# Classical FFN weights: the remainder made by a negation on ScalarE and an accumulating transfer

## The chip, the cores and the metric

The kernel runs on one core of one Trainium2 chip. A core has five engines with a queue of instructions each: TensorE (PE in the profile, with its weight loads as PEld), VectorE (DVE), ScalarE (ACT), GpSimd (POOL) and SyncE (SP). Each queue is worked off in order, and the engines wait for one another through semaphores. DMA transfers are issued from the queues of SP, ACT or POOL and run on 16 DMA engines that all queues share. Data lies in SBUF (128 partitions); matrix products land in PSUM.

The metric is the time of one execution on the device in microseconds (us), lower is better; of several runs the median is taken.

## The reference

One decoder layer on x of 512 tokens by 1024 features, in float32: a half-step SwiGLU feed-forward block, a mixing block with a diagonal state-space model beside sliding-window attention, a second half-step SwiGLU block and a final RMS norm.

```python
def swiglu(h, w_gate, w_up, w_down):
    return (jax.nn.silu(h @ w_gate) * (h @ w_up)) @ w_down

x = x + 0.5 * swiglu(rms_norm(x, ffn1_norm), ffn1_w_gate, ffn1_w_up, ffn1_w_down)
...
x = x + y @ w_out
x = x + 0.5 * swiglu(rms_norm(x, ffn2_norm), ffn2_w_gate, ffn2_w_up, ffn2_w_down)
return rms_norm(x, final_norm)
```

`w_gate` and `w_up` are 1024 by 2816, `w_down` is 2816 by 1024: 22 blocks of 128 columns or rows.

## The kernel before

**Three products for one.** PE multiplies in a format with fewer bits than float32 (fp32r). So every operand is split into a high part, rounded to fp32r, and a remainder, operand minus high part, and `mm3` adds three products into one PSUM tile: weight-high by x-high (L182), weight-high by x-remainder (L183), weight-remainder by x-high (L184).

**Weights.** `weight` (L175) takes a tile of 128 partitions by up to 1024 columns: eight blocks of 128 by 128 for a gate or up column block, six or five for a down tile. `weight_part` (L169) loads it from SP's queue into `wraw`, casts it on ScalarE into `whi` (L154, inside `copy`), and has DVE subtract `whi` from `wraw` into `wlo` (L173). Each of the three names has three buffers, so the cast of a tile waits until PE has read `whi` of the tile three before for the last time, and the load of a raw tile until the buffer of the tile three before has been read by L173. A gate or up tile is 24 matmuls, a down tile 18 or 15.

**Who calls it.** `weight` and `weight_part` have an argument `key`. The mixing block passes a name for each of its weights (`u0`, `wkv1`, `out00` and so on), and a table of engines, `ENGINES`, sends a few of these splits to GpSimd. The feed-forward blocks pass nothing, so `key` is the empty string: in the first block all 44 gate and up tiles and 32 down tiles, in the second block the 12 tiles of the first six column blocks and 24 down tiles. The remaining ten column blocks of the second block go another way (`pairs`, with its own cast L536, subtraction L537 and sums on GpSimd L502), and so does the last group of its down tiles. `start` (L288) loads x and the first gate and up tile in three cuts each, by calling `weight_part` itself.

**What else runs beside it.** In the first feed-forward block, after each tile one step of a list (`prep_steps`) is put into the program. These steps prepare the state-space matrices: short operations on DVE, then two long chains of products and sums on GpSimd (`tt` with the engine G, all at L635), one for `aB`, which PE later transposes (`tV`, L830, four empty steps behind the chain), and one for `matC`, which is read much later, in the mixing block. Before the last column blocks of the second feed-forward block, GpSimd adds weight blocks (`s`, L502) for `pairs`.

**The order.** The source writes a tile's load, cast and subtraction just ahead of its matmuls. The framework's planner reorders the instructions with a simulated timeline: an instruction goes into its engine's queue when the planner reckons it ready, earlier in the source first. It allots buffers, and adds the semaphore waits. On the chip each queue then runs in that fixed order.

Of the kernel before, what the change touches and what calls it, by code (L numbers as in the profile page):

```python
# [10 lines left out]
F32 = mybir.dt.float32  # L11
# [3 lines left out]
ALU = mybir.AluOpType  # L15
AX = mybir.AxisListType

P = 128
# [116 lines left out]
class Body:  # L135
# [33 lines left out]
    def weight_part(self, tiles, src, c0, c1, key=""):  # L169
        raw, hi, lo = (t[:, c0:c1] for t in tiles)  # L170
        self.nc.sync.dma_start(raw, src[:, c0:c1])
        self.copy("hi" + key, hi, raw)
        self.eng("lo" + key).tensor_tensor(lo, raw, hi.bitcast(F32), op=ALU.subtract)  # L173

    def weight(self, src, cols, key=""):  # L175
        t = self.weight_tiles()
# [3 lines left out]
    def mm3(self, out, wh, wl, xh, xl, start, stop, **kw):  # L180
        mm = self.nc.tensor.matmul
        mm(out, wh, xh, start=start, stop=False, **kw)  # L182
        mm(out, wh, xl, start=False, stop=False, **kw)  # L183
        mm(out, wl, xh, start=False, stop=stop, **kw)  # L184
        if self.small:
            self.small.pop(0)()
# [101 lines left out]
    def start(self):  # L288
        nc = self.nc
        self.prenorm(self.g_ffn1)  # L290
        self.x = [self.cp.tile([P, 512], F32, name=f"x{k}") for k in range(KT)]
        src = self.d["wgu1"][0]
        ws = [self.weight_tiles() for _ in range(2)]
        cuts = {0: (0, 2), 2: (2, 5), 5: (5, 8)}
        for k in range(KT):
            nc.sync.dma_start(self.x[k], self.d["xT"][k])
            if k in cuts:
                for gu in range(2):
                    self.weight_part(ws[gu], src[gu].rearrange("p k m -> p (k m)"), cuts[k][0] * P, cuts[k][1] * P)
            self.xg.append(self.split_gain(self.x[k], self.g_ffn1[:, k:k + 1]))  # L300
        self.first = [(w[1], w[2]) for w in ws]

# [1235 lines left out]
```

## Time and profile before

| | us |
|---|---|
| median of 3 runs | 935.81 |
| lowest and highest run | 926.32, 936.68 |
| span of the profiled execution | 925.4 |
| the profiled execution's own time (span and what lies around it) | about 926.3 |

The profiled execution's time is taken to be that of the run next to its span. The profile is one execution. Its page gives the busy time of each engine, the span in 40 slices, the chain of work that ended last, the costliest groups of instructions by line, and the DMA issues; a group's last column is the idle time of its engine ahead of it and what ended that. The trace behind it answers questions for one engine, tile, line or stretch of time, always in microseconds from the start of the span; "L173" is line 173 of the kernel, and "x3" means three instructions in one row. A matmul's row is longer (0.39 us) than the distance to the next (0.23 us), since matmuls overlap.

### The profile page before, as it was taken

The page shows a single profiled execution, that of the slowest core. Times are in us where ns is not written, and L with a number is a line of the kernel's source. Part 1 is how long each engine was busy: PE and PEld are TensorE (multiplying, and loading weights), DVE is VectorE, ACT ScalarE, POOL GpSimd, SP SyncE. Part 2 cuts the span into 40 slices and gives each one's busy share as a digit, 9 for nine tenths or more (in the row PEclk, how much of TensorE's full clock was granted, in tenths as well). Part 3 has the DMA queues.
Part 4 walks back from the last instruction along what each step waited for, and adds up shares of the span by engine and source line. Part 5 has one row for each costly group of instructions (what it writes and reads, how often), then busy time and mean ns, then how long its engine had stood idle before and what let it go on. Part 6 is the DMA issues. An engine that isn't in the chain of part 4 may idle for free.

```text
span 925.4 us, 13303 instructions
## 1 busy us (share of the span) xinstructions
PE 907.5 (98%) x5036; PEld 772.9 (84%) x5036; DVE 624.0 (67%) x1167; ACT 369.2 (40%) x660; POOL 314.9 (34%) x272
## 2 busy tenths in 40 slices
PE   9999999999999999999979999999999999999996
PEld 6887888888888888888868887888899889988995
DVE  7886444474464443958896787697588459855966
ACT  7142233222232322622487433543355335532553
POOL 0009902179950000501231063180553055404502
PEclk9999999999999999999989999999999999999998
DMA  7332423243213321547201122215421442135112
GB/s 244 125 92 53 153 91 103 64 133 121 84 57 112 114 76 56 164 149 186 78 1 46 46 79 104 91 36 157 150 86 35 134 156 87 35 110 180 47 47 91
DMA packets 37503, 91.92 MB, mean 99 GB/s; under 512 B 8032, under 2 KB 10304, under 8 KB 37184
## 3 DMA queue, kind: packets, MB, share of 16 engines
q1 hardware_dynamic: 37008, 90.54, 31.3%
q8 instruction: 39, 0.64, 0.3%
q10 hardware_dynamic: 432, 0.55, 0.2%
q14 instruction: 24, 0.20, 0.1%
HBM read 87.44 MB, written 3.64 MB: 98 GB/s over the span
## 4 chain that ended last, share of the span: by engine, by line
PE 91%; DVE 5%; ACT 2%; issue 1%; DMA 1%; SPq 0%; DVEq 0%; ACTq 0%
PE gu L182 11%; PE gu L183 11%; PE gu L184 11%; PE dn L182 9%; PE dn L183 8%; PE dn L184 8%; PE gua L184 3%; PE gua L183 3%; PE gua L182 3%; PE guc L184 2%; PE guc L182 2%; PE guc L183 2%; PE ow L182 2%; PE ow L183 2%; PE ow L184 2%; PE pt L1037 1%
## 5 line engine op out<-in xcount | busy, mean ns | idle before, releaser
L154 ACT CAST whi<-wraw 128x1024 fp32r<-128x1024 f32 (+4 forms) x134 | 122.6, 921 | 307.6 <-PE gu L183 118.9
L173 DVE TENSOR_TENSOR wlo<-wraw,whi 128x1024 fp32r<-128x1024 f32 (+4 forms) x133 | 155.4, 1173 | 42.6 <-ACT whi L154 42.5
L182 PE MATMUL gu<-hi,whi 128*128 128x512 f32 x448 | 178.9, 402 | 1.5 <-ACT hi L195 1.4
L183 PE MATMUL gu<-lo,whi 128*128 128x512 f32 x448 | 176.7, 395 | 0.1
L184 PE MATMUL gu<-hi,wlo 128*128 128x512 f32 x448 | 176.3, 395 | 0.0
L183 PE MATMUL dn<-lo,whi 128*128 128x512 f32 (+1 forms) x336 | 130.1, 389 | 0.0
L182 PE MATMUL dn<-hi,whi 128*128 128x512 f32 (+1 forms) x336 | 130.1, 392 | 0.0
L184 PE MATMUL dn<-hi,wlo 128*128 128x512 f32 (+1 forms) x336 | 128.9, 389 | 0.0
L182 PEld LDWEIGHTS gu<-hi,whi 128*128 128x128 f32 x448 | 84.4, 189 | 21.8 <-ACT hi L195 2.3
L184 PEld LDWEIGHTS gu<-hi,wlo 128*128 128x128 f32 x448 | 84.3, 188 | 19.7
L183 PEld LDWEIGHTS gu<-lo,whi 128*128 128x128 f32 x448 | 84.5, 189 | 19.2 <-DVE lo L197 1.0
L182 PEld LDWEIGHTS dn<-hi,whi 128*128 128x128 f32 x336 | 63.3, 188 | 14.9 <-ACT whi L154 1.1
L184 PEld LDWEIGHTS dn<-hi,wlo 128*128 128x128 f32 x336 | 63.2, 188 | 14.2
L183 PEld LDWEIGHTS dn<-lo,whi 128*128 128x128 f32 x336 | 63.3, 188 | 13.6
L269 POOL TENSOR_TENSOR sq<-sq 128x512 f32<-128x512 f32 x17 | 25.1, 1476 | 139.9 <-ACT sq L265 137.2
L537 DVE TENSOR_TENSOR wlo<-s,whi 128x512 fp32r<-128x512 f32 x64 | 55.2, 904 | 12.2 <-ACT whi L536 12.0
L502 POOL TENSOR_TENSOR s<-s,wraw 128x512 f32<-128x512 f32 x32 | 50.4, 1576 | 33.9 <-DMA wraw<-wgs 32.9
L502 POOL TENSOR_TENSOR s<-wb 128x512 f32<-128x512 f32 x16 | 23.6, 1474 | 112.3 <-DMA wb<-wgs 91.4
L345 DVE TENSOR_TENSOR u<-gu,R 128x512 f32<-128x512 f32 x28 | 19.2, 685 | 48.2 <-PE gu L184 48.2
L412 DVE SCALAR_TENSOR_TENSOR x<-dn,x 128x512 f32<-128x512 f32 x32 | 21.7, 685 | 42.7 <-PE dn L184 42.7
L536 ACT CAST whi<-s 128x512 fp32r<-128x512 f32 x64 | 36.5, 618 | 30.4 <-issue 9.3
L428 DVE SCALAR_TENSOR_TENSOR x<-dn,x 128x512 f32<-128x512 f32 x24 | 16.5, 690 | 46.2 <-PE dn L184 46.2
(371 smaller groups left out, 2030.1 us busy)
## 6 DMA issues: line engine op xcount, KB each, us to landing
wraw<-wgu SPq DMA_DIRECT2D x54, 512.0 KB, 3.4
wraw<-wd SPq DMA_DIRECT2D x40, 384.0 KB, 3.2
wb<-wgs SPq DMA_DIRECT2D x32, 256.0 KB, 5.2
wraw<-wgs SPq DMA_DIRECT2D x16, 512.0 KB, 3.7
wraw<-wd SPq DMA_DIRECT2D x16, 320.0 KB, 2.9
wraw<-wout SPq DMA_DIRECT2D x8, 512.0 KB, 3.4
x<-xT SPq DMA_DIRECT2D x8, 256.0 KB, 5.1
wraw<-wu SPq DMA_DIRECT2D x4, 512.0 KB, 3.3
```

Of the source, the lines that this page charges most:

```text
L154: (e.copy if e is self.nc.scalar else e.tensor_copy)(out, x)
L173: self.eng("lo" + key).tensor_tensor(lo, raw, hi.bitcast(F32), op=ALU.subtract)
L182: mm(out, wh, xh, start=start, stop=False, **kw)
L183: mm(out, wh, xl, start=False, stop=False, **kw)
L184: mm(out, wl, xh, start=False, stop=stop, **kw)
L269: (eng or b.nc.gpsimd).tensor_tensor(self.acc, self.acc, sq, op=ALU.add)
L345: nc.vector.tensor_tensor(u, pu, self.R, op=ALU.mult)
L412: nc.vector.scalar_tensor_tensor(self.x[m], ps, 0.5, self.x[m], op0=ALU.mult, op1=ALU.add)
L428: self.nc.vector.scalar_tensor_tensor(self.x[m], ps, 0.5, self.x[m], op0=ALU.mult, op1=ALU.add)
L502: add = lambda o, x, y: nc.gpsimd.tensor_tensor(o, x, y, op=ALU.add)
L536: self.chained("A", lambda: A.copy(hi[:, c], w))
L537: self.chained("V", lambda: V.tensor_tensor(lo[:, c], w, hi[:, c].bitcast(F32), op=ALU.subtract))
```

## The change

For tiles with an empty `key`, the remainder is no longer a subtraction on DVE. ScalarE, which has just written `whi`, reads it again and writes its negative into `wlo`. Then a DMA from GpSimd's queue moves `wraw` into `wlo` and adds it to what stands there: minus the high part, plus the raw weight. The first two tiles, which `start` loads in cuts, get the key `"0"`, and so keep cast and subtraction as they were. The weights of the mixing block have keys of their own and are unchanged, as is the path through `pairs`. So 110 tiles change: 54 of 1024 columns, 40 of 768 and 16 of 640.

```diff
@@ weight_part
         self.copy("hi" + key, hi, raw)
-        self.eng("lo" + key).tensor_tensor(lo, raw, hi.bitcast(F32), op=ALU.subtract)
+        if key:
+            self.eng("lo" + key).tensor_tensor(lo, raw, hi.bitcast(F32), op=ALU.subtract)
+        else:
+            self.nc.scalar.mul(lo, hi.bitcast(F32), -1.0)
+            self.nc.gpsimd.dma_start(lo, raw, accum_op=ALU.add)
@@ start
-                    self.weight_part(ws[gu], src[gu].rearrange("p k m -> p (k m)"), cuts[k][0] * P, cuts[k][1] * P)
+                    self.weight_part(ws[gu], src[gu].rearrange("p k m -> p (k m)"), cuts[k][0] * P, cuts[k][1] * P, "0")
```

## The prediction

> **What bounds the kernel now.** I read the page first (busy shares, slices, chain of work, groups, DMA issues).
>
> ```profile
> span 925.4 us, 13303 instructions
> PE 907.5 (98%) x5036; PEld 772.9 (84%) x5036; DVE 624.0 (67%) x1167; ACT 369.2 (40%) x660; POOL 314.9 (34%) x272
> ...
> POOL 0009902179950000501231063180553055404502
> ...
> PE 91%; DVE 5%; ACT 2%; issue 1%; DMA 1%; SPq 0%; DVEq 0%; ACTq 0%
> ...
> L154 ACT CAST whi<-wraw 128x1024 fp32r<-128x1024 f32 (+4 forms) x134 | 122.6, 921 | 307.6 <-PE gu L183 118.9
> L173 DVE TENSOR_TENSOR wlo<-wraw,whi 128x1024 fp32r<-128x1024 f32 (+4 forms) x133 | 155.4, 1173 | 42.6 <-ACT whi L154 42.5
> ...
> wraw<-wgu SPq DMA_DIRECT2D x54, 512.0 KB, 3.4
> wraw<-wd SPq DMA_DIRECT2D x40, 384.0 KB, 3.2
> ...
> wraw<-wd SPq DMA_DIRECT2D x16, 320.0 KB, 2.9
> ```
>
> PE is busy 98% and is 91% of the chain: only 17.9 us of the span are not matmul, so no relief of another engine is worth more than that. GpSimd, 34% on average, is nearly full in slices 3, 4 and 9, 10 (23 us each): the first feed-forward block. Then I read whom PE and the DMA queue wait for.
>
> ```profile
> PE pt L1329 <- ACT pr L1308: 4.7, 1, 4.7
> ...
> PE gua L184 <- DVE wlo L537: 0.3, 1, 0.3
> ...
> SPq L171 <- DVE wlo L173: 492.9, 104, 32.3
> ```
>
> PE loses nothing to L173. The loads of raw weights wait on it 104 times: a raw buffer comes free when its remainder is made. That is where the lead of a weight tile is set, and it reads from the casts, each released by PE's last L183 on the tile three before.
>
> ```profile
> 199.53 0.83 ACT L154 CAST whi<-wraw 128x768 fp32r<-128x768 f32 x1 [3.36 <-PE dn L183]
> 203.69 0.84 ACT L154 CAST whi<-wraw 128x768 fp32r<-128x768 f32 x1 [3.32 <-PE dn L183]
> ...
> 231.69 1.05 ACT L154 CAST whi<-wraw 128x1024 fp32r<-128x1024 f32 x1 [4.55 <-PE gu L183]
> 237.29 1.05 ACT L154 CAST whi<-wraw 128x1024 fp32r<-128x1024 f32 x1 [4.54 <-PE gu L183]
> ...
> 291.41 0.73 ACT L154 CAST whi<-wraw 128x640 fp32r<-128x640 f32 x1 [3.65 <-PE dn L183]
> 294.43 0.73 ACT L154 CAST whi<-wraw 128x640 fp32r<-128x640 f32 x1 [2.29 <-PE dn L183]
> ```
>
> PE takes 5.6 us for a gate/up tile (1024 columns), 4.2 for a down tile of six blocks (768), and here 3.0 for one of five (640). With three buffers a cast begins two tiles ahead of PE's need, plus about 0.7 us (the last L184 and the two matmuls before the next first one): a lead of 11.9, 9.1 and 6.7 us. Today cast and subtraction fill about 2.2 us of it.
>
> **What is removed and added.** 54 + 40 + 16 = 110 subtractions leave DVE, at most 129 us at the group's mean of 1.17. PE does not get them: it waits for none of them above. ScalarE gains 110 negations of the cast's size, 54 x 1.05 + 40 x 0.84 + 16 x 0.73 = 102 us on an engine busy 40%: hidden, except that each lengthens the way to its remainder. A negation needs the remainder's buffer, free at PE's last L184, one matmul after the cast's release and long before the cast ends, so it adds no wait of its own; the casts and Silus behind it on ScalarE come 0.7 to 1.05 us later, and of these one is in the sum below. The first two tiles keep the DVE form. What matters is the new transfer: no row shows an accumulating one, or any DMA from GpSimd.
>
> ```profile
> L171 SPq DMA_DIRECT2D wraw<-wd x56: 327/328/949, 50.9 to 828.1; - x56
> ...
> L173 POOL TENSOR_TENSOR wlo<-wraw,whi 128x1024 fp32r<-128x1024 f32 x3 | 7.4, 2466 | 42.6 <-ACT whi L154 42.4
> ...
> matT<-dz SPq DMA_DIRECT2D x2, 1024.0 KB, 8.3
> ...
> 206.00:267.00 61.00, 61.00 (x263) 49.05 (x263) 30.73 (x30) 15.33 (x18) 60.92 (x44) 1.00 0.31 94
> ```
>
> Its issue lies between 0.33 us (SP's) and 2.47 (a GpSimd pass over the tile); I take the middle, 1.4, since GpSimd has no hardware issue in this trace to be nearer to. Its transfer lies between the plain load (3.4 us for 512 KB) and the slowest row with twice the bytes, 8.3. An add must read its destination as well, so I take twice the bytes at the loads' slope: from 320 to 512 KB they grow 0.5 us, 1.3 us per 512 KB, giving 4.7, 4.2 and 3.7 us. DMA is 31% busy, worth 0.5; a cast or Silu ahead on ScalarE 0.6. From the end of the negation that is an estimate of 7.2, 6.7 and 6.2 us (bounds 3.7 and 11). What is left of the lead after cast and negation is 9.8, 7.4 and 5.2: hidden by 2.6 and 0.7, and 1.0 us short for tiles of five blocks. On "Collectives: The Full Stack" (section on the bandwidth ceiling) the Trainium skill says that a DMA reduction runs at about half the rate of a copy because it reads two sources; no run here shows it yet. With plain loads' transfer instead the terms below marked * vanish, and the sum would be about 12 instead of 24.
>
> The raw loop also grows: cast 0.84, negation 0.84, 6.7, SP's issue 0.33, load 3.2 is 11.9 us against three tiles of 12.6. It holds, barely. SP's queue is in order, so what stands behind a waiting raw load (the x tiles, the pair weights of the second block) waits too; in the paired stages that is the load that L502 needs.
>
> **Start.** The third tile is the first new one.
>
> ```profile
> 14.55 1.05 ACT L154 CAST whi<-wraw 128x1024 fp32r<-128x1024 f32 x1 [0.59 <-DMA wraw<-wgu]
> ...
> 18.57 0.39 PE L184 MATMUL gu<-hi,wlo 128*128 128x512 f32 x1
> ```
>
> Cast to 15.6, negation to 16.65, plus 7.2 is 23.85, and PE wants it at 18.57: 5.3 late, or 1.6 if the planner moves the eight L184 behind the sixteen others of the tile. I take 4.
>
> **GpSimd's queue.** Its work is in order, so each issue delays the work behind it, and each waits for what is ahead.
>
> ```profile
> 70.50 0.62 POOL L635 TENSOR_TENSOR tB<-sB,p_zi 128x256 f32<-128x256 f32 x1
> 71.08 1.34 POOL L635 TENSOR_TENSOR tB<-sB,p_zr 128x256 f32<-128x256 f32 x1
> ...
> 113.22 1.45 POOL L635 TENSOR_TENSOR aB<-tB 128x256 f32<-128x256 f32 x2
> 115.11 0.60 PE L830 MATMUL tV<-cst,aB 128*128 128x128 f32 x4
> ...
> 220.97 1.06 POOL L635 TENSOR_TENSOR tC<-matC,s_ar 128x512 f32<-128x512 f32 x1
> 221.58 1.54 DVE L173 TENSOR_TENSOR wlo<-wraw,whi 128x1024 fp32r<-128x1024 f32 x1 [0.16 <-ACT whi L154]
> 221.99 2.04 POOL L635 TENSOR_TENSOR tC<-Y,s_ai 128x512 f32<-128x512 f32 x1
> ```
>
> The chain that builds aB runs from about 70 to 114.67, and PE's transposes read it at 115.11: 0.4 us of slack. Ten tiles fall into that stretch: 10 x 1.4 = 14 us of issues. Against it stands what DVE gives back: beside L173 a GpSimd operation stretches (1.06 to 2.04 us; 0.62 to 1.34), so ten vanished subtractions return about 7. The chain ends 7 later and PE waits for it, in order, unless its transposes are moved: I take 6. The Trainium skill ("SBUF — State Buffer", who interferes with whom) has the rule behind that give-back, that a DVE instruction with two SBUF inputs blocks a GpSimd one that reads SBUF; the rows agree.
>
> The second burst (206 to 267, 60.92 us busy) has no reader soon. But some eight down tiles of six blocks fall into the two bursts, and their transfers queue behind operations of 1 to 2 us: half an operation, 0.8, uses up the 0.7 of margin, and behind two of them a tile is 2 late: 4* in all. An issue that stands ahead of its negation's end holds back everything behind it; the planner puts it where it reckons it ready, so I count none (rival D). The sixteen tiles of five blocks are 1.0 short, paid once per three buffers, and each wait counts again: 16 x 0.33 = 5*.
>
> **Second block.** Down tiles after the two paired stages:
>
> ```profile
> 717.21 0.83 ACT L154 CAST whi<-wraw 128x768 fp32r<-128x768 f32 x1 [0.19 <-PE gua L183]
> ...
> 723.30 0.40 PE L184 MATMUL dn<-hi,wlo 128*128 128x512 f32 x1
> ...
> 796.31 1.75 POOL L502 TENSOR_TENSOR s<-s,wraw 128x512 f32<-128x512 f32 x1
> 798.54 0.69 DVE wlo L537
> ```
>
> Negated at 718.9, plus 6.7 is 725.6 against 723.3: 2.3 late, twice, 5*. The sums of L502 feed a piece of the chain itself (798.54); a transfer placed among them costs its issue once or twice: nothing if none is, 3 at most, I take 0.
>
> Sum: 4 + 6 + 4 + 5 + 5 = 24 us. The profiled execution is its span plus about 0.9, 926.3, the fastest run shown; the median, 935.81, lies 9.5 above. 926.3 + 24 + 9.5 = 960.
>
> **Rivals.** (B) The transfer outlasts the lead everywhere. At one and a half times the estimate (10.8, 10.0, 9.3) the excess over 9.8, 7.4 and 5.2, shared by three buffers, is 54 x 0.33 + 40 x 0.87 + 16 x 1.4 = 75 us more, about 1030. For it: both unknown prices are software or double traffic; against it: the upper bound needs 8.3, a transfer of strided 1 MB. (C) It is hidden anyway: the estimate lies below the lead if the transfer costs what a load costs and the issue no more than the returned 0.7 us. Then only the start remains, or nothing: 930 to 945; not slower. It decides at a remainder landing 7.4 us after the negation in six-block tiles. It can hardly be faster: PE's 17.9 idle us lie outside the changed lines. (D) The planner, which writes GpSimd's order, reckons with the unhindered 1.06 us; in the 61 us burst 44 operations take 60.92, or 1.38, so the last transfers stand 14 us too far back, and beyond the margin of 2.6 PE waits 11 more: 971. PE loses nothing to GpSimd today, which speaks neither way, for nothing PE wants soon is queued there now.
>
> **How the numbers follow.** My sum has 0.45 (its own range 945 to 980), B 0.20, C 0.27, D 0.08. About 2% is what a measurement can tell, 917 to 954.5. The sum falls below 954.5 with 0.12, C is faster with 0.02: faster 0.02, same 0.25 + 0.12 = 0.37, slower 0.61. From 934 (a third of C is left out) to 1020 (half of B) is eight in ten.
>
> **What would show it.** Time from the negation's end to landing near 7 us; PE idle in front of L184 released by that transfer, most in tiles of five blocks and after the paired stages; a wait of about 6 us at the transposes of aB; GpSimd's operations near 1.05 us; SP waiting on the new transfers instead of DVE. I am wrong if a transfer lands in under 5 us, if PE's order is rewritten around late remainders, or if waits at GpSimd's other work exceed 10 us.

## The result and the profile after

| us | before | after |
|---|---|---|
| median of 4 runs | 935.73 | 976.19 |
| lowest and highest run | 926.32, 936.68 | 975.14, 976.4 |
| span of the profiled execution | 925.4 | 974.5 |

The kernel before has two usual times, near 926 and near 936 us, and now and then one near 956; its profiled execution is one near 926. The changed kernel is slower: the ratio of the times is 1.0473, with a 95% interval of 1.0416 to 1.0531. Its lines below the edit carry numbers 4 higher: the negation is L176, the transfer L177, the keyed subtraction L174, `mm3` L186 to L188, the sums L506, the chains of GpSimd L639. The page of the changed kernel, its busy shares, its chain of work, the new groups and the DMA issues (the last column there is the median time from issue to landing):

```profile
span 974.5 us, 13624 instructions
PE 922.8 (95%) x5036; PEld 778.9 (80%) x5036; DVE 543.8 (56%) x1057; ACT 465.7 (48%) x770; POOL 374.2 (38%) x382
...
PE 60%; DMA 14%; POOL 8%; issue 7%; DVE 6%; ACT 3%; SPq 0%; POOLq 0%; DVEq 0%; ACTq 0%
...
L177 POOL DMA_DIRECT2D wlo<-wraw x110 | 100.2, 915 | 339.5 <-ACT wlo L176 324.1
...
wraw<-wgu SPq DMA_DIRECT2D x54, 512.0 KB, 4.5
wlo<-wraw POOLq DMA_DIRECT2D x54, 512.0 KB, 5.7
...
wlo<-wraw POOLq DMA_DIRECT2D x40, 384.0 KB, 4.7
wraw<-wd SPq DMA_DIRECT2D x16, 320.0 KB, 3.1
wlo<-wraw POOLq DMA_DIRECT2D x16, 320.0 KB, 4.0
```

DVE lost 80 us of busy time and ScalarE took on 97. But PE's share of the chain fell from 91% to 60%, and the new chain runs through the DMA engines, GpSimd and DVE. To see where the 49.1 us of span lie, cut both executions at the same numbers of finished matmuls. First the windows of before, then those of the changed kernel (length of the window, then busy time and number of instructions of PE, PEld, DVE, ACT and POOL, the granted clock, the DMA share and GB/s):

```profile
0.00:50.70 50.70, 48.53 (x200) 36.65 (x201) 41.70 (x179) 22.99 (x34) 1.48 (x8) 1.00 0.53 174
50.70:141.90 91.20, 91.19 (x401) 73.23 (x400) 53.75 (x96) 27.50 (x36) 45.72 (x49) 1.00 0.31 96
141.90:272.30 130.40, 130.40 (x601) 106.75 (x600) 69.63 (x105) 33.03 (x42) 85.53 (x81) 1.00 0.32 97
272.30:318.90 46.60, 46.60 (x202) 37.63 (x201) 20.48 (x27) 11.55 (x15) 0.00 (x0) 1.00 0.33 108
318.90:562.00 243.10, 236.40 (x1402) 199.37 (x1401) 173.88 (x377) 109.39 (x223) 50.80 (x40) 0.99 0.29 88
562.00:925.40 363.40, 354.40 (x2237) 319.30 (x2235) 264.61 (x387) 164.74 (x311) 131.41 (x95) 0.99 0.30 97
```

```profile
0.00:58.55 58.55, 52.95 (x200) 40.04 (x201) 41.12 (x212) 32.48 (x45) 8.00 (x16) 0.94 0.76 205
58.55:158.60 100.05, 93.83 (x401) 75.05 (x401) 41.97 (x37) 42.05 (x51) 49.46 (x66) 0.97 0.76 170
158.60:293.40 134.80, 131.43 (x602) 106.62 (x601) 47.51 (x72) 51.24 (x59) 87.99 (x105) 1.00 0.78 180
293.40:349.70 56.30, 49.16 (x201) 38.18 (x200) 15.80 (x25) 24.61 (x32) 9.56 (x12) 0.97 0.73 161
349.70:594.10 244.40, 236.68 (x1402) 199.11 (x1401) 158.96 (x364) 122.48 (x240) 63.88 (x56) 0.99 0.45 116
594.10:974.50 380.40, 358.75 (x2237) 319.95 (x2235) 238.42 (x351) 192.85 (x344) 155.26 (x129) 0.99 0.51 133
```

The differences of the lengths are 7.9 (start), 8.9 (GpSimd's first burst), 4.4 (its second), 9.7 (the tiles of five blocks), 1.3 (the last of these and the mixing block) and 17.0 us (second feed-forward block): together 49.1. PE's busy time grew as well, by 15.3 us. About 8 of them are the clock, whose column is below 1.00 where PE stopped: PE was busy at half clock for 22.4 us in this execution and for 6.0 in the one before, and half of the difference is lost. The other 7 are not explained here. Whom PE waited for (total, times, longest), and then whom ScalarE's casts and SP's loads waited for, all in the changed kernel:

```profile
PE dn L188 <- DMA wlo<-wraw: 17.6, 15, 3.0
PE gu L188 <- DMA wlo<-wraw: 7.3, 5, 2.7
PE dn L187 <- DVE lo L209: 5.2, 1, 5.2
```

```profile
ACT whi L154 <- DMA wraw<-wgu: 34.6, 10, 9.9
ACT whi L154 <- DMA wraw<-wd: 29.1, 8, 7.6
```

```profile
SPq L171 <- DMA wlo<-wraw: 519.2, 101, 17.0
```

PE waits for the transfer 20 times, 24.9 us in all, and once, 5.2 us, for DVE; six waits for late casts (L186) add 3.4 us. With the 15.3 us of longer busy time that is 48.8 of the 49.1 us. ScalarE waits 63.7 us for raw weights; before, its waits for these loads came to 0.9 us in all, since a raw buffer then came free with DVE's subtraction. Now it comes free when the transfer has landed.

Four places show how a remainder comes late. At the start, other work of ScalarE stands between cast and negation (timeline of the changed kernel):

```profile
14.38 1.05 ACT L154 CAST whi<-wraw 128x1024 fp32r<-128x1024 f32 x1 [0.59 <-DMA wraw<-wgu]
...
15.34 4.27 ACT L269 ACTIVATE sq<-x 128x512 f32<-128x512 f32 x8
...
19.52 1.04 ACT L176 ACTIVATE wlo<-whi 128x1024 fp32r<-128x1024 f32 x1
...
20.86 1.00 POOL L177 DMA_DIRECT2D wlo<-wraw  x1 [20.42 <-ACT wlo L176]
```

Eight squares of the norm, 4.27 us, come first; PE's L188 starts 5.1 us after that issue and has waited 1.96 us for the landing. Just before, PE had waited 1.81 us for the next cast, which stands behind the negation on ScalarE. In GpSimd's first burst it is DVE that is late (windows of the changed kernel):

```profile
92.00:97.40 5.40, 0.18 (x1) 0.00 (x0) 5.36 (x1) 0.00 (x0) 4.80 (x7) 0.87 0.45 105
97.40:99.00 1.60, 1.59 (x4) 1.31 (x5) 0.33 (x1) 0.76 (x1) 0.00 (x0) 0.50 0.05 10
...
101.00:103.00 2.00, 2.00 (x7) 1.59 (x6) 0.00 (x0) 0.41 (x1) 2.00 (x3) 0.56 0.34 65
103.00:106.00 3.00, 3.00 (x14) 2.34 (x13) 0.69 (x1) 1.40 (x2) 1.21 (x2) 1.00 0.93 170
```

One DVE instruction fills the window from 92.0 to 97.4, GpSimd runs without a gap until 96.8, and PE does nothing. The clock falls to half during the stop, at 95.95, and stays there for 6.8 us, 5.4 of them after PE has resumed. The instruction is L209, which forms the remainder of the hidden activations; its timeline row reads

```profile
90.58 6.78 DVE L209 TENSOR_TENSOR lo<-a,hi 128x512 fp32r<-128x512 f32 x1 [0.81 <-POOL aB L639]
...
273.17 16.20 DVE L209 TENSOR_TENSOR lo<-a,hi 128x512 fp32r<-128x512 f32 x1 [0.76 <-ACT hi L207]
```

where its 28 instances took 0.76 us on average in the kernel before. Among the tiles of five blocks three casts come in a bunch. The kernel before has this bunch too (timeline of ScalarE before, then of the changed kernel):

```profile
285.40 1.35 ACT L154 CAST whi<-wraw 128x640 fp32r<-128x640 f32 x2 [5.93 <-PE dn L183]
287.03 0.73 ACT L154 CAST whi<-wraw 128x640 fp32r<-128x640 f32 x1 [0.28 <-ACT whi L154]
```

```profile
299.16 0.71 ACT L154 CAST whi<-wraw 128x640 fp32r<-128x640 f32 x1
308.94 1.36 ACT L154 CAST whi<-wraw 128x640 fp32r<-128x640 f32 x2 [4.82 <-PE dn L187]
310.84 0.71 ACT L154 CAST whi<-wraw 128x640 fp32r<-128x640 f32 x1
320.36 0.73 ACT L154 CAST whi<-wraw 128x640 fp32r<-128x640 f32 x1 [7.55 <-DMA wraw<-wd]
```

So the change does not make the bunch; what follows it is new. Before, each subtraction takes 0.8 us and PE waits for none of them; the next raw loads are issued at 287.64, 288.37 and 289.70, and the cast at 291.41 finds its weights there. In the changed kernel the three transfers land at 314.88, 316.71 and 319.42, PE stops for 2.59 us in front of the first, and the next raw loads are issued right behind these landings, at 314.93, 316.76 and 319.47. So the cast at 320.36 has waited 7.55 us for its raw weights. Finally, in the second block an issue stands behind other work of GpSimd (timeline of the changed kernel):

```profile
686.71 0.85 ACT L176 ACTIVATE wlo<-whi 128x768 fp32r<-128x768 f32 x1
...
690.51 1.29 POOL L506 TENSOR_TENSOR s<-s,wraw 128x512 f32<-128x512 f32 x1 [5.51 <-DMA wraw<-wgs]
...
694.70 0.86 POOL L177 DMA_DIRECT2D wlo<-wraw  x1
...
698.62 0.50 PE L188 MATMUL dn<-hi,wlo 128*128 128x512 f32 x1 [3.02 <-DMA wlo<-wraw]
```

The negative is ready at 687.56, but the transfer is issued at 694.70, because the sums ahead of it in GpSimd's queue waited 5.51 us for raw weights of their own. The landing then took 3.9 us, less than the median. The same happens at 892.07, with a PE stop of 2.6 us.

### The profile page after: what moved, and what is told of

Its sections match the earlier page's. It is cut to its first block, busy times and chain, and to the rows that moved or that the text cites. A ratio compares the mean times of both kernels' runs of the same rounds, so it can differ in the third digit from the quotient of the medians.

```text
span 974.5 us, 13624 instructions
## 1 busy us (share of the span) xinstructions
PE 922.8 (95%) x5036; PEld 778.9 (80%) x5036; DVE 543.8 (56%) x1057; ACT 465.7 (48%) x770; POOL 374.2 (38%) x382
## 4 chain that ended last, share of the span: by engine, by line
PE 60%; DMA 14%; POOL 8%; issue 7%; DVE 6%; ACT 3%; SPq 0%; POOLq 0%; DVEq 0%; ACTq 0%
DMA wlo<-wraw 10%; PE gu L188 7%; PE gu L186 7%; PE gu L187 7%; PE dn L188 4%; PE dn L187 3%; PE dn L186 3%; PE gua L188 3%; PE gua L187 3%; PE gua L186 3%; PE guc L188 2%; PE guc L187 2%; PE guc L186 2%; POOL tC L639 1%; DVE lo L209 1%
## 5 line engine op out<-in xcount | busy, mean ns | idle before, releaser
L177 POOL DMA_DIRECT2D wlo<-wraw x110 | 100.2, 915 | 339.5 <-ACT wlo L176 324.1
L188 PE MATMUL gu<-hi,wlo 128*128 128x512 f32 x448 | 178.0, 400 | 7.4 <-DMA wlo<-wraw 7.3
L186 PE MATMUL gu<-hi,whi 128*128 128x512 f32 x448 | 180.3, 405 | 2.9 <-ACT whi L154 2.9
L188 PE MATMUL dn<-hi,wlo 128*128 128x512 f32 (+1 forms) x336 | 133.0, 402 | 17.7 <-DMA wlo<-wraw 17.6
L187 PE MATMUL dn<-lo,whi 128*128 128x512 f32 (+1 forms) x336 | 132.6, 396 | 5.2 <-DVE lo L209 5.2
L186 PE MATMUL dn<-hi,whi 128*128 128x512 f32 (+1 forms) x336 | 132.4, 397 | 0.5 <-ACT whi L154 0.5
L188 PEld LDWEIGHTS gu<-hi,wlo 128*128 128x128 f32 x448 | 85.6, 191 | 29.4 <-DMA wlo<-wraw 9.6
L186 PEld LDWEIGHTS gu<-hi,whi 128*128 128x128 f32 x448 | 85.6, 191 | 24.0 <-ACT whi L154 5.6
L176 ACT ACTIVATE wlo<-whi 128x1024 fp32r<-128x1024 f32 (+2 forms) x110 | 102.0, 932 | 2.2
L188 PEld LDWEIGHTS dn<-hi,wlo 128*128 128x128 f32 x336 | 64.7, 192 | 38.3 <-DMA wlo<-wraw 24.4
L186 PEld LDWEIGHTS dn<-hi,whi 128*128 128x128 f32 x336 | 64.5, 192 | 14.8 <-ACT whi L154 1.6
L209 DVE TENSOR_TENSOR lo<-a,hi 128x512 fp32r<-128x512 f32 x28 | 55.9, 1996 | 24.5 <-ACT hi L207 23.7
L506 POOL TENSOR_TENSOR s<-s,wraw 128x512 f32<-128x512 f32 x32 | 48.4, 1514 | 15.6 <-DMA wraw<-wgs 14.6
```

Source lines behind the costliest of these rows:

```text
L176: self.nc.scalar.mul(lo, hi.bitcast(F32), -1.0)
L177: self.nc.gpsimd.dma_start(lo, raw, accum_op=ALU.add)
L209: nc.vector.tensor_tensor(lo, x, hi.bitcast(F32), op=ALU.subtract)
L506: add = lambda o, x, y: nc.gpsimd.tensor_tensor(o, x, y, op=ALU.add)
```

## The experiments

Theory: what costs is that the remainder, and with it the free raw buffer, comes later than the lead that three buffers leave, because of the transfer's own time and of what stands ahead of it on ScalarE's and GpSimd's queues. First rival: the parts cost by themselves, whoever waits for them: the negation, or the load on GpSimd and the DMA engines. Second rival: the 5.2 us stop and its like, DVE instructions held back by a busier GpSimd, are the main loss. The kernels ran on three chips, and each ratio is to the kernel before on the same chip, whose median there was 935.3, 927.02 or 935.59 us.

| kernel | median (lowest to highest), us | ratio to before, 95% interval |
|---|---|---|
| negation, DVE adds, no transfer | 952.92 (937.53 to 962.46) | 1.0119 (0.9999 to 1.024) |
| DVE remainder, transfer into a spare tile | 965.51 (962.16 to 977.66) | 1.0363 (1.0274 to 1.0451) |
| the same, plain copy | 955.7 (one run) | none |
| the change with four weight buffers | 950.15 (949.82 to 951.22) | 1.0213 (1.0134 to 1.0293) |
| before with four weight buffers | 935.49 (933.0 to 949.48) | 1.0057 (1.001 to 1.0105) |
| the change on gate and up tiles alone | 944.34 (936.3 to 945.31) | 1.0154 (1.008 to 1.0228) |
| the change without the second block's down tiles | 959.41 (954.95 to 960.3) | 1.0296 (1.0212 to 1.038) |
| the change without the first three column blocks | 967.8 (966.52 to 969.92) | 1.0404 (1.0337 to 1.0471) |
| before, one copy in each chain step | 928.96 (927.55 to 930.16) | 0.9992 (0.9959 to 1.0025) |
| before, two copies in each chain step | 934.76 (932.43 to 943.33) | 1.0055 (1.0009 to 1.0102) |
| the change, one copy in each chain step | 973.8 (971.79 to 976.73) | 1.0496 (1.0444 to 1.0548) |

### The negation without the transfer

The negation stays on ScalarE, and DVE adds the raw weight:

```diff
             self.nc.scalar.mul(lo, hi.bitcast(F32), -1.0)
-            self.nc.gpsimd.dma_start(lo, raw, accum_op=ALU.add)
+            self.nc.vector.tensor_tensor(lo, raw, lo.bitcast(F32), op=ALU.add)
```

> ScalarE still negates the high part into the remainder's buffer, but DVE adds the raw weight; no transfer. Lead theory (the transfer lands later than the two-tile lead allows) and queue theory (GpSimd's queue and what it does to DVE): all of the loss is gone, 926 to 940 us. If the negation on ScalarE is what costs: above 950.

Measured 952.92 us, with a spread of 25 us. The profiled execution, 959.83 us, is near the upper end of it; in its timeline one row of DVE stands out:

```profile
93.18 16.84 DVE L177 TENSOR_TENSOR wlo<-wraw,wlo 128x768 fp32r<-128x768 f32 x3 [0.97 <-ACT wlo L176]
```

Three additions take 16.84 us beside GpSimd's chain, and end with it; PE waits 15.2 us for them, and no more than 1.9 us for any other product of the changed lines. By its number alone the median falls under "above 950", where the negation was to be what costs. The profile says otherwise: cut at the same numbers of matmuls, 17 of the 33 us that this execution is longer than the one before lie in the stretch with this stop, and 3 at the start, where PE waits 1.9 us for a cast that stands behind a negation. Some 10 more lie in the mixing block, where PE runs at half clock for 20.5 us without a stop (521.98 to 542.46); no run ties that to the negation. The fastest run, 937.53, is 11.6 us above the fastest of the kernel before on that chip, and it was not profiled. So the negations cost PE a few us where a wait shows them, and what they cost beyond that stays open. This bears on the second rival: DVE can be held long enough to stop PE without any transfer.

### The transfer without anyone who waits for it

DVE makes the remainder as before, and GpSimd's transfer adds the raw weights to one of two spare tiles that nobody reads (the pool `m2p` has 39 buffers in place of 43, to make room):

```diff
-            self.nc.scalar.mul(lo, hi.bitcast(F32), -1.0)
-            self.nc.gpsimd.dma_start(lo, raw, accum_op=ALU.add)
+            self.nc.vector.tensor_tensor(lo, raw, hi.bitcast(F32), op=ALU.subtract)
+            self.spare.reverse()
+            self.nc.gpsimd.dma_start(self.spare[0][:, c0:c1], raw, accum_op=ALU.add)
```

> DVE makes the remainder as before the change, and GpSimd issues the same accumulating transfer, from the raw buffer into a spare tile that nobody reads (two spare tiles, paid for by four activation buffers fewer). Lead theory: nobody waits for the copy, so 926 to 940 us. Queue theory: GpSimd's 110 issues still hold up its own work and DVE's reads, 940 to 955, and DVE instructions of several us stand beside GpSimd's chains. If the load on the DMA engines costs: raw loads land as late as in the changed kernel (about 4.5 us for 512 KB) and it is above 955.

> The kernel in which VectorE makes the remainder and GpSimd's queue moves the raw weights into spare tiles that nobody reads, now with a plain copy in the place of the accumulating transfer. If the add doubles the work of the transfer (its destination is read as well), the median from issue to landing of 512 KB falls from 5.9 us to 4.0 to 4.7 us, beside about 5 us of the raw loads in the same kernel. If GpSimd's queue and the number of transfers set it, it stays at 5.5 to 5.9 us. The time of the whole is by the first 955 to 962 us, by the second 965 us as before.

With the accumulating transfer 965.51 us, with a plain copy in its place (the edit is `accum_op` left out) 955.7. The DMA issues of the first and of the second kernel:

```profile
wraw<-wgu SPq DMA_DIRECT2D x54, 512.0 KB, 5.0
spare<-wraw POOLq DMA_DIRECT2D x54, 512.0 KB, 5.9
```

```profile
wraw<-wgu SPq DMA_DIRECT2D x54, 512.0 KB, 3.7
spare<-wraw POOLq DMA_DIRECT2D x54, 512.0 KB, 3.1
```

The same 512 KB from the same queue land after 5.9 us with the add and after 3.1 without it, more of a fall than was expected, and the raw loads beside them fall from 5.0 to 3.7. So the add itself, not GpSimd's queue, makes the transfer long, and it slows the loads that share the DMA engines. On "Collectives: The Full Stack" (section on the bandwidth ceiling) the Trainium skill puts the reducing step of a ring collective at about half the rate of the copying one, since the add reads two sources; 3.1 against 5.9, here for a plain transfer, agrees. The issue costs less as well, 0.55 against 0.91 us on average. Of the 28 us by which the profiled execution with the plain copy is longer than that of the kernel before, 16 lie in the stretch where DVE is held again (timeline of that kernel; its L210 is L209 of the changed kernel, and PE waited 11.4 us for it), and 11 in the second block:

```profile
88.31 12.32 DVE L210 TENSOR_TENSOR lo<-a,hi 128x512 fp32r<-128x512 f32 x1 [0.68 <-ACT hi L208]
```

The clock is at half from 89.15 to 106.22. With the additions, time and raw loads are as expected if the load on the DMA engines costs. But in neither of the two kernels does PE wait for a DMA: it waits some 25 us (additions) and 19 us (copies) for DVE and, behind DVE, for ScalarE. So the first rival holds for the additions, which cost this kernel some 30 us even where nobody waits for them, as far as PE's waits show by way of DVE. For the copies it is not shown: 955.7 is one run, and the kernel before had one of 955.78 on that chip. How far this adds to the late remainders is not read from these two kernels, since here DVE still carries the subtractions.

### More buffers

The changed kernel, and the kernel before as a control, with four buffers of each weight tile in place of three (`m2p` 37):

```diff
-        self.wp = ctx.enter_context(tc.tile_pool(name="wp", bufs=3))
+        self.wp = ctx.enter_context(tc.tile_pool(name="wp", bufs=4))
```

> The changed kernel with four buffers for each of the three weight tiles (six activation buffers fewer). Lead theory: a lead of three tiles hides the transfer, what is left is the start and the DVE stall, 940 to 955 us. Queue theory: stays above 960, since an issue that stands behind other work of GpSimd, and DVE's waits, do not depend on the number of buffers.

> Control for the four buffers: the kernel before with the same four weight buffers and six activation buffers fewer. All theories: as before, 924 to 940 us.

The changed kernel falls to 950.15, the control stays at 935.49 (both on one chip): the loss shrinks from 40 to 15 us. In the changed kernel with four buffers PE waits for the transfer 8.0 us instead of 24.9; the larger part of it is

```profile
PE dn L188 <- DMA wlo<-wraw: 6.1, 5, 2.3
```

The transfers are not faster there (6.3 us for 512 KB); only the lead is longer. That is the theory's main point; the first rival by itself would have left the time where it was. Cut at the same numbers of matmuls, the profiled execution loses against its control 5.3 us at the start, 2.6 in the first burst, 5.3 among the tiles of five blocks and 0.5 in the second block, where the changed kernel lost 7.9, 8.9, 9.7 and 17.0. ScalarE no longer waits for the raw weights of any down tile.

### Which tiles

Three kernels take the change back for some of the tiles, by giving them a key: all 56 down tiles; the 24 down tiles of the second block; the gate and up tiles of the first three column blocks.

```diff
-                wh, wl = self.weight(wd[m, :, f0:f1].rearrange("p k m -> p (k m)"), nf * P)
+                wh, wl = self.weight(wd[m, :, f0:f1].rearrange("p k m -> p (k m)"), nf * P, "d")
...
-                    wh, wl = self.weight(wgu[f, gu].rearrange("p k m -> p (k m)"), 1024)
+                    wh, wl = self.weight(wgu[f, gu].rearrange("p k m -> p (k m)"), 1024, "s" if f < 3 else "")
```

> The changed kernel, with the 56 down tiles back on DVE: only the 54 gate and up tiles use the transfer. Lead theory: these have 2.6 us to spare, so the start (8 us) and little else remains, 938 to 950 us. Queue theory (every issue on GpSimd costs alike): about half of the loss, 950 to 958.

> The changed kernel with the 24 down tiles of the second block put back on VectorE's subtraction; the 86 other tiles keep negation and transfer. Lead theory (a remainder that comes later than the lead that two weight buffers leave): nearly all of the 14 to 15 us by which PE fell behind after 590 us are waits of these tiles, so this run gives 961 to 964 us and no PE wait of dn on a wlo DMA after 590 us. Rival, contention (GpSimd and the DMA engines are busier whatever the tile): the second block's loss turns into waits elsewhere, and the run stays at 972 us or above.

> The changed kernel with the tiles of the first three column blocks of the first block's gate and up weights put back on VectorE's subtraction; all other tiles keep negation and transfer. Start theory: the 7.9 us by which PE fell behind in the first 31 us of the changed kernel are the eight squares between cast and negation and the wait for the landing, so this run gives about 968 us (976 less 7.9), with no PE wait on a wlo DMA before 31 us. Rival, the give-back of later waits: the time made up at the start is lost again where the remainders come late anyway, and the run stays at 974 to 976 us.

The change on gate and up tiles alone gives 944.34, as the lead theory expected: half of the tiles, and by the ratios a third of the loss (1.5% of 4.7%). In its profile PE waits for a transfer four times, 2.4 us in all. Its loss is the start, 7.4 us, and the stretch of GpSimd's first burst, 7.0, where a DVE product (L351) of 14.37 us holds up ScalarE and, through it, PE for 4.2. Without the second block's down tiles it is 959.41, somewhat below the 961 to 964 expected, and PE waits for no transfer of a down tile after 590 us; the last window of that kernel, beside 363.4 us before and 380.4 after, is

```profile
593.65:958.40 364.75, 354.79 (x2238) 319.33 (x2236) 257.74 (x375) 173.12 (x320) 135.86 (x105) 0.99 0.38 113
```

so 24 of 110 tiles carried 15.65 of the 17.0 us lost there, and none of it came back elsewhere in the block. Without the first three column blocks it is 967.8, where 968 was expected; the first window, beside 50.7 before and 58.55 after, is

```profile
0.00:50.10 50.10, 48.03 (x201) 36.52 (x202) 41.36 (x194) 27.68 (x39) 4.21 (x11) 1.00 0.65 199
```

The start's loss is gone whole, and the half clock with it (1.00 against 0.94). The rest of that execution loses nearly as much as the changed kernel's, 40 against 41 us: in its stretch from 50.1 to 147.8 us the DVE stop is missing, and three transfers that were issued 7 to 8 us behind their negations, stops of 4.9 us together, stand in its place.

### DVE beside a GpSimd that never pauses

The second rival is tested from both sides: in each step of GpSimd's two chains DVE copies one column of the step's input into the step's first product tile, so that GpSimd must wait for DVE once per step and a held DVE instruction can start. The copies are put into the kernel before and into the changed one (`GAP`, the empty steps behind the chain, is 5 in place of 4), and the kernel before is profiled once more.

```diff
                 t2 = S.m2(name="tB2")
+                V.tensor_copy(t[:, 0:1], y[:, 0, 0:1])
...
+                V.tensor_copy(t[0][:, 0, 0:1], y[:, 0, 0:1])
```

> The kernel before, once more, for a second profile: its times lie near 926 or near 936 us. Starvation theory (a DVE instruction with two SBUF inputs waits until GpSimd's run of back-to-back instructions ends, in some executions and not in others): an execution near 936 shows one DVE instruction of more than 5 us inside 70 to 115 us, one near 926 shows none. If the two times have another cause: no such instruction in either.

> The kernel before, with GpSimd made to wait once per step of its two chains for a one-column copy on DVE (and one more empty step ahead of the transposes, GAP 5). Starvation theory: no DVE instruction is held longer than one step (about 5 us in the first chain, 7 in the second), every run lies near 926 to 930 us, and the runs near 936 are gone. Otherwise: the same two levels as before, or some us slower for the longer chains.

> The changed kernel with the same yields in GpSimd's chains. Starvation theory: the 5.2 us stop of PE near 92 us and the slow clock behind it are gone, 964 to 970 us, and the rest of the loss stays (start, late remainders). Lead theory alone: 974 to 978.

> The kernel before with two one-column VectorE copies in each step of GpSimd's chains in the place of one, on which GpSimd waits, so that a held VectorE instruction can start twice as often. Theory that the levels of 926, 935 and 956 us of the kernel before are VectorE instructions held through GpSimd's back-to-back work: all runs within 926 to 930 us, none near 935. Rival (the levels have another cause): runs near 935 us are there again. If each copy costs more than it frees, 930 to 935 us in all runs.

The kernel before ran at 926.33, and no DVE instruction in it lasted over 2.6 us; its other 14 runs on that chip lay in three groups, nine at 926 to 928, four at 935 to 936 and one at 956.5. With one copy per step all ten runs lie between 927.55 and 930.16: the higher groups are absent and the time is the same (ratio 0.9992, 0.9959 to 1.0025). If 5 runs in 14 usually lie higher, ten without one are about a 1% chance; but this kernel also has `GAP` 5, which was not run alone. With two copies per step they lie between 932.43 and 943.33, against the expectation. There DVE waits for GpSimd by semaphore, with PE behind it (timeline of the kernel with two copies):

```profile
88.88 0.16 DVE L816 COPY tB<-aB 128x1 f32<-128x1 f32 x1 [2.88 <-POOL aB L635]
```

DVE's queue is in order, so a copy that waits 2.88 us for GpSimd holds up the activations behind it, and PE stands for 6.4 us until ScalarE has cast them (L203). So here the copies cost more than they free. The runs of this kernel also speak against held DVE instructions as the cause of the step from 926 to 936 us: three of them lie 10 us above three others (942.4 to 943.3 against 932.4 to 932.9) although GpSimd pauses twice in each step, at a mean granted clock of 0.979 against 0.991. In the kernel before the step of 10 us goes with a clock of 0.982 to 0.986 against 0.992 to 0.994. A clock lower by 0.012 over 930 us is an estimated 22 us at half clock, which costs some 11 us of work: the whole step, with no engine stopped. The profile of the negation without the transfer has such a stretch (20.5 us in the mixing block). That the slower runs of the kernel before have it too is likely, but not shown, since none of them was profiled.

In the changed kernel the copies remove the 5.2 us stop, and the stretch of the first burst shrinks from 100.2 to 96.9 us. The median, 973.8, lies just below the lead theory's 974 to 978 and above the 964 to 970 of the starvation theory; its ratio of 1.0496 is no lower than the changed kernel's 1.0473. PE waits for transfers as before, 25.8 us; the larger part is

```profile
PE dn L188 <- DMA wlo<-wraw: 20.4, 13, 3.9
```

So the second rival is a real mechanism, but in the changed kernel it is worth some 3 us of that stretch and nothing that is clear of noise in the whole: take the held instruction away, and a late remainder in the same place, 2.85 us, is the next wait.

No version tried here beats the kernel before.

## Why the prediction was right or wrong

It foresaw a loss and took the late remainder as its cause, and both held. The size was half: 24 us in the sum against 49.1 in the spans. That 960 was no further from 976.19 than 16 us is due to the 9.5 us it added for the way from the profiled execution to the median, and that was luck. The changed kernel has no such way: its runs lie within 1.3 us, and its profiled run, 976.28, is at the median.

**The transfer's time: too high.** From the negation's end to landing the prediction took 7.2, 6.7 and 6.2 us. The usual distance to the issue is 0.3 us, and from issue to landing 5.7, 4.7 and 4.0 pass: 6.0, 5.0 and 4.3. The doubled traffic was right (3.1 against 5.9 above), the issue of 1.4 us was 0.92. The prediction said that it would be wrong if a transfer landed in under 5 us; the smaller ones do, and the kernel is slower all the same. So the condition was badly chosen: it looked at the transfer alone. Without the terms marked * the sum is 10 us, not "about 12".

**The lead: the step that failed.** The prediction read the leads of 11.9, 9.1 and 6.7 us from casts with even spacing and gave them to every tile. But the kernel before casts its down tiles in bunches at two places, three at 87.00 and three at 285.40, and a tile in a bunch has much less. A subtraction of 0.8 us fitted in there; a transfer of 4 us did not. Behind the bunch the raw loop, of which the prediction said for six blocks that "It holds, barely", passes the delay on. It was not worked out for five: with the prediction's own figures it is 0.73, 0.73, 6.2, 0.33 and 2.9, or 10.9 us, against three tiles of 3.0. As measured, cast 0.73, negation 0.73, 0.3 to the issue, 4.0 to landing, SP's issue 0.33 and load 3.1 are 9.2 us: only 0.2 too long, so the loop alone does not make the loss, but it leaves no time to catch up. The 63.7 us that ScalarE waited for raw weights show it, most plainly the cast at 320.36. The window of these tiles lost 9.7 us instead of 5, 2.7 of them at the gate and up tile behind them. Four buffers, which lengthen the lead and loosen this loop, took back some 25 of 40 us; 5.3 of the 9.7 stayed, and so did the bunch (four casts there, from 298.10 to 301.34).

**Start: mechanism right, size off.** 7.9 instead of 4. The prediction took the negation to follow its cast at once; ScalarE did eight squares of 4.27 us first, PE waited 1.81 us for the cast behind the negation, which the sum for the start left out, and lost clock at its stops. Taking the three column blocks back returned 8.4 us.

**Transposes of aB: no wait.** The 6 us were put at the wrong place. GpSimd's chain did end later, at 119.5 instead of 114.7, but PE was late itself by then (16.7 us at the end of the second window) and reached the transposes at 122.93. Also the give-back failed: without DVE's subtractions beside it the chain's operations were no faster (those that write aB: 0.96 us before, 1.14 after). And GpSimd stood for 6.5 us in that stretch in front of two issues whose negation was not ready, which the prediction counted as none. Instead DVE was held in that stretch, which lost 8.9 us, most of it by the stop and the half clock; the prediction did not have that. The rule it cited there from the Trainium skill ("SBUF — State Buffer", who interferes with whom) was used in one direction only; the same section says that the issue order decides which of the two is blocked, and here it was DVE.

**Six-block tiles in the bursts.** 4 was predicted and 4.4 measured in the second burst; one remainder there was issued 5.2 us after its negation, behind chain operations, more than the half operation reckoned.

**Second block: size off.** 5 predicted, 17.0 measured, 15.65 of it by the down tiles. The prediction counted two tiles 2.3 us late and nothing for the sums of L502. Two of the largest stops, 3.0 and 2.6 us, are transfers queued 7.1 and 7.0 us behind those sums. That is the mechanism of rival D (the planner's place for the issue, then 0.08), in another part of the kernel than D put it. Three others there are landings 6 to 8 us after the issue, beside the loads for the sums.

**Rivals.** B, the transfer outlasting the lead everywhere, did not happen: beside 54 gate and up tiles alone PE waited 2.4 us for transfers. C, hidden but for the start, did not happen with three buffers.

## What to carry to other kernels

The lead has to be read where the casts stand closest together, not where they are evenly spaced. A buffer's loop has to be added up for every tile size, the smallest above all: when a short engine step becomes a transfer, the buffer that it reads is held until the landing, and the next load starts that much later. A DMA issue on an engine's queue is as late as everything ahead of it there, so look for operations that themselves wait for loads, and count their waits, not only their work. If such a move must be made, give it one more buffer, and leave the tiles with the least lead on the old path.

## What the runs showed of the hardware

A DVE subtraction of two SBUF tiles, 0.76 us on average in the kernel before, lasted 16.20 us beside GpSimd operations that followed each other without a pause, and 12.32 us in another kernel. In both profiles of the kernel before, and in both of it with the copies, no DVE instruction lasted over 2.6 us.

By the clock records of all profiles here, half clock comes in stretches of 3.41 us or whole multiples of it (6.83, 10.24, 17.07, 20.48), but for the one at the end of the span, and within one profile their starts lie whole multiples of 3.41 us apart. So a stretch does not begin where a stop begins or ends: in the changed kernel it began 3.8 us into the stop of 5.2 us, 0.5 us before the end of one of 2.6 us (314.40), and 1.5 us after the end of one of 3.0 us (700.11). Two other stops of 2.6 and 2.7 us left the clock at 1.00, so the length of a stop alone did not decide. Cutting each profile into these 3.41 us pieces, from 12 us on, shows more: every piece at full clock in which PE stood still for 1.92 us or more was followed by half clock, none with less than 0.93 us was, and in between both happened. What ends half clock stays open: the stretch of 20.5 us in the kernel with the negation alone lasted although PE did not stop.
